# A state-space and mLSTM decoder block on one core: one rotation table for four batches, an earlier weight ring, and weight sums laid out by rows

## The chip, the core and the metric

The kernel runs on one core of a Trainium2 chip. The core has a matrix engine (TensorE, PE in the profile, with PEld for the loading of its weights), VectorE (DVE), ScalarE (ACT), GpSimd (POOL) and SyncE (SP), and 16 DMA engines that move data between the chip's main memory and on-chip memory. Each engine works its instructions in program order and waits on semaphores for the others. The metric is the device time of one execution, in microseconds (us).

## What is computed

One decoder block on 1024 positions of width 1024, with 16 learned positions in front, all in float32. Cut to what matters:

```python
h = layer_norm(concat([meta, x]), ln0_g, ln0_b)
p = h @ w_in + b_in
u_s5, q, k, v, o_pre, i_pre, f_pre, g_s5, g_m = split(p)
y_s5 = s5(u_s5, ...)                      # 32 groups x 64 complex states: x_t = A x_{t-1} + B u_t, y_t = Re(C x_t) + D u_t
z = gelu(y_s5) @ s5_w_glu
y_s5 = z[:, :1024] * sigmoid(z[:, 1024:])
...
y_m = (sigmoid(o_pre) * head_norm(mlstm(conv_silu(q, k), v, i_pre, f_pre))) @ m_w_out
mix = sigmoid(g_s5) * y_s5 + sigmoid(g_m) * y_m
h = layer_norm(alpha * h + mix @ w_o)
h = layer_norm(alpha * h + relu(h @ w_up + b_up) ** 2 @ w_down)
```

## The kernel before

**Matrix products.** Every float32 product is made of three passes (mm3, L226 to L228): both operands are split into a high part, rounded to the PE's fast format, and a low part, the remainder. For a weight tile of 128 x 1024 the load is L198 (wraw, from SP), the high part whi is a copy by ACT (L212) and the low part wlo a subtraction by DVE (L213). The first pass uses whi (L226), the second whi with the low part of the input (L227), the third wlo (L228).

**Jobs.** The first half of the block is a list of jobs, ORDER: q and k, v, o (output gates of the mLSTM), u (input of the state-space layer S5, four jobs u0 to u3), g (gates of S5), m (two of the mLSTM's gate tiles), and then z0 to z7 (the GLU product on gelu(y_s5)). A job is one or two weight tiles and some 48 matmuls; weights are loaded two jobs ahead and split one job ahead, with high priority. The rest of the gates (three pairs of tiles) and the mLSTM's output product come after z7 as stages of seven products in place of eight (class Seven), then the output projection, a layer norm and the feed-forward part.

**Side work.** S5, mLSTM, convolution and the residual scaling are generators in lanes ("s5c", "s5", "s5g", "ml", "cv", "ah"); mm3 pumps them between matmuls by a running estimate of PE time, and a yield states what a step is thought to cost. A scheduler then sets the order of the instructions on each engine, by priorities; from there each engine goes through its own queue in order, so an instruction that stands late in DVE's queue waits for all ahead of it.

**S5.** The 32 groups run as four batches b of four group pairs (q runs over 16 pairs). When the job of S5_START begins, s5_pre computes powers of the transition. When job u_b is done, s5_consts(b) and s5_batch(b) are queued. s5_consts builds the input and output matrices (L699 to L741) and a table T of 130 rotations for each of its four pairs, by doubling: seven complex products of 4, 8, 16, 32, 64, 128 and 256 columns and one more of 4, each of six DVE operations (cmul, L572 to L577, through the tile s5tt). s5_batch multiplies the input by a matrix (L802, PE), copies the result out (L810), rotates it by T (L817 to L823), runs the recurrence as a scan (L828), rotates back (L838 to L841), puts the halves together (L846) and multiplies by the output matrix (L857, L858, PE). The result goes through main memory (ys_dr, L863; s5yc, L871), and s5_gelu applies gelu and splits it into gelh and gell (L877, L878), which z0 to z7 multiply.

**Residual scaling and early up-projection.** At job g4 ah_scale is queued (ahr in by L1377, two DVE products L1386, out by L1388), and behind it up_early, which computes a part of the feed-forward weights' combinations (L1412, L1413) and stores them (wu_dr, L1414).

**The seam after z7.** When z7 begins, the pool mid is closed and a pool ring is opened in its place, with three buffers of two weight tiles for the stages of seven products. begin() issues eight loads of the normalised input (rawb, L991). After z7, first() loads three ring buffers (Seven.load, L1024), splits the first (Seven.split: whi L1042, wlo L1043) and forms the sums and differences of input blocks (sub, L1002; to_home, L997 and L998). Four of the seven products need sums of weight blocks; w_sums has POOL's DMAs compute them in main memory (ws_dr, L974), one DMA in every second job, some adding into the destination.

Of the kernel before, what the change touches and what calls it, by code (L numbers as in the profile page):

```python
# [38 lines left out]
LN2_2 = math.log(2.0) - LN2_1  # L39
MAGIC = 1.5 * 2 ** 23  # L40
ORDER = "q0 q1 v0 q2 v1 q3 o1 o0 v2 o2 o3 u0 u1 v3 u2 g0 u3 g1 o4 o5 o7 o6 g2 g3 g5 g6 g4 g7 m0 m1"
S5_START = "u0"
NM = 2
SPLIT_UP = 200
PRE = 3
# [67 lines left out]
def decoder_block(  # L113
# [80 lines left out]
    def load_w(job):  # L194
        job.raw = []
        for src, n in job.loads:
            r = slot("wraw") if ring[0] is None else ring[0].tile([P, 1024], F32, tag="wr", bufs=3, name="wraw")
            nc.sync.dma_start(r[:, :n], src)  # L198
            job.raw.append(r)

# [378 lines left out]
    def s5_pre():  # L579
# [89 lines left out]
             v3(tm[:, 0:256]), v3(tm[:, 256:512]))  # L669
        yield 1.3  # L670

    GEL = {}

    def s5_consts(b):
# [83 lines left out]
                g_.dma_start(mx[16 * j:16 * j + 16, :, g2, 16 * j:P],  # L758
                              kt[16 * g2:16 * g2 + 16, :, 0:P - 16 * j])
        yield K5[b]  # L760
        T = slot("s5T")
        tc_, ts_ = (T[:, i * 520:(i + 1) * 520].rearrange("p (q c) -> p q c", q=4) for i in range(2))
        tmp = slot("s5tt")
        g_.memset(tc_[:, :, 0], 1.0)
        g_.memset(ts_[:, :, 0], 0.0)
        g_.tensor_copy(tc_[:, :, 1], S5["p8"][:, 0, q0:q0 + 4])
        g_.tensor_copy(ts_[:, :, 1], S5["p8"][:, 1, q0:q0 + 4])
        yield C5[b]
        n = 1
        while n < 129:  # L770
            m = min(n, 129 - n)
            sh = [P, 4, m]
            w1 = tmp[:, 0:4 * m].rearrange("p (q c) -> p q c", q=4)
            w2 = tmp[:, 512:512 + 4 * m].rearrange("p (q c) -> p q c", q=4)
            cmul(v_, tc_[:, :, n + 1:n + 1 + m], ts_[:, :, n + 1:n + 1 + m], tc_[:, :, 1:m + 1], ts_[:, :, 1:m + 1],
                 tc_[:, :, n:n + 1].to_broadcast(sh), ts_[:, :, n:n + 1].to_broadcast(sh), w1, w2)
# [181 lines left out]
    def w_sums():  # L958
        todo = {}
        for s, (n0, p0, w, i0) in enumerate(((3, 0, wf, JGM + NM), (4, 3, wmo, 0))):  # L960
            def src(r, kh):
                return bass.AP(tensor=w.tensor, offset=w.offset + (i0 + r) * KT * P * P + 512 * kh,
                               ap=[[2 * KT * P * P, n0], [KT * P, P], [1, 512]])
            a11, a12, a21, a22 = src(0, 0), src(0, 1), src(1, 0), src(1, 1)
            d = [ws_dr[p0:p0 + n0, i] for i in range(4)]
            todo[s] = [(d[0], a21, 0), (d[2], a11, 0), (d[0], a22, 1), (d[2], a21, 1), (d[1], d[0], 0), (d[1], a11, 1),
                       (d[3], d[1], 0), (d[3], a12, 1)]
        mark = const.tile([1, 1], F32, name="mark")
        for s, i in ((0, 0), (0, 1), (0, 2), (0, 3), (0, 4), (1, 0), (0, 5), (1, 1), (0, 6), (1, 2), (0, 7), (1, 3),
                     (1, 4), (1, 5), (1, 6), (1, 7)):  # L970
# [33 lines left out]
    class Seven:  # L1004
# [8 lines left out]
        def load(self, i):  # L1013
            if i >= self.ntile():
                return
            r = ring[0].tile([P, 1024], F32, tag="wr", bufs=3, name="wraw")
            for j, (n, p) in enumerate(self.units[2 * i:2 * i + 2]):
                s = {5: 0, 6: 1, 7: 2, 3: 3}.get(n)
                if s is None:
                    t = self.w[self.i0 + 2 * p + (n == 4)].rearrange("p k f -> p (k f)")  # L1020
                    a = t[:, 0:512] if n == 1 else t[:, 512:1024]
                else:
                    a = ws_dr[self.p0 + p, s]
                tc.keep_in_program_order(nc.sync.dma_start(r[:, j * 512:j * 512 + 512], a))  # L1024
            self.raw[i] = r
# [117 lines left out]
    def gates_and_output():  # L1143
# [6 lines left out]
            for nm, kh, ch in (("12", 0, 1), ("22", 1, 1), ("11", 0, 0), ("21", 1, 0)):  # L1150
                R[nm] = raw_block(h_dr, kh, ch, META)

        def first():
            for i in range(3):
                g.load(i)
            g.split(0)
            sub(R["22"], R["12"], R["22"])
            sub(R["12"], R["12"], R["11"])
# [919 lines left out]
```

## Time and profile before

| | before |
|---|---|
| median of 3 runs | 1566.78 us (1564.85 to 1566.83) |
| profiled execution | 1566.04 us, span 1564.2 us |
| mean granted clock of TensorE | 0.984 |
| matmuls | 7593 |
| DVE instructions | 2083 |

The span is what the profiler recorded between the first and the last instruction; 1.84 us of that execution lie around it. A row of the page by slices cuts the span in 40 equal parts of 39.1 us and gives busy tenths of each engine:

```profile
PE   8999999998999998989999999999999999999997
DVE  7667555659867845677789675666666679766786
PEclk9999999998999999989999999999999999999999
DMA  8412324414354556775353328644443798667642
```

The granted clock falls to 0.8 in the tenth slice (352 to 391 us) and in the eighteenth (665 to 704 us), and PE's busy share is lowest there and in the sixteenth (587 to 626 us). The windows further on look into these three places.

### The profile page before, as it was taken

What the parts mean: (1) busy time and instruction counts of PE and PEld (TensorE: products, weight loads), DVE (VectorE), ACT (ScalarE), POOL (GpSimd) and SP (SyncE); (2) the same over time, 40 slices, a digit from 0 to 9 for tenths busy, and PEclk for the clock granted to TensorE, in tenths of its full rate; (3) what the DMA queues carried; (4) which work ended last, traced back from release to release, by engine and by line L of the source; (5) the groups of instructions that cost most, each with busy time, mean ns of one, the idle gap of its engine ahead of it and who ended that gap; (6) DMA issues with size and microseconds to landing.
All of it is one profiled execution on the core that took longest, in us unless ns stands there. A gap on an engine that the chain in (4) does not pass through costs nothing.

```text
span 1564.2 us, 20543 instructions
## 1 busy us (share of the span) xinstructions
PE 1515.8 (97%) x7593; PEld 1278.7 (82%) x7593; DVE 1079.9 (69%) x2083; ACT 642.7 (41%) x982; POOL 102.2 (7%) x195
## 2 busy tenths in 40 slices
PE   8999999998999998989999999999999999999997
PEld 8998988996878886768788887888888888888886
DVE  7667555659867845677789675666666679766786
ACT  6523353333355433325534324444444534433340
POOL 0000001124031200000000001000000000000000
PEclk9999999998999999989999999999999999999999
DMA  8412324414354556775353328644443798667642
GB/s 311 159 57 61 100 62 129 122 37 112 104 129 103 164 182 218 279 269 195 108 170 114 108 76 247 225 158 149 147 149 123 248 363 322 230 229 236 216 166 108
DMA packets 137509, 261.32 MB, mean 167 GB/s; under 512 B 30768, under 2 KB 52984, under 8 KB 137352
## 3 DMA queue, kind: packets, MB, share of 16 engines
q1 hardware_dynamic: 111344, 233.00, 43.7%
q0 software_dynamic: 26064, 27.01, 7.1%
q8 instruction: 60, 0.98, 0.3%
q14 instruction: 41, 0.34, 0.1%
HBM read 188.78 MB, written 84.55 MB: 175 GB/s over the span
## 4 chain that ended last, share of the span: by engine, by line
PE 31%; issue 23%; DMA 3%; DVE 2%; ACT 0%; SPq 0%; POOL 0%; POOLq 0%; DVEq 0%
PE mm L228 7%; PE mm L227 7%; PE mm L226 7%; PE sd L227 3%; PE sd L226 3%; PE sd L228 3%; DMA wpre<-wu_dr 1%; DMA rawb<-h_dr 1%; DMA wu_dr<-wpre 1%; DMA wur<-in_wup_dram 0%; DVE wlo L1043 0%; DVE wlo L213 0%; DMA woraw<-in_wo_dram 0%; POOL wpre L1621 0%; SPq L991 0%
## 5 line engine op out<-in xcount | busy, mean ns | idle before, releaser
L226 PE MATMUL mm<-hT_hi,whi 128*128 128x512 f32 (+3 forms) x604 | 231.0, 382 | 8.0 <-ACT whi L1042 5.4
L228 PE MATMUL mm<-hT_hi,wlo 128*128 128x512 f32 (+3 forms) x604 | 226.7, 380 | 5.7 <-DVE wlo L213 3.7
L227 PE MATMUL mm<-hT_lo,whi 128*128 128x512 f32 (+3 forms) x604 | 229.1, 379 | 0.0
L226 PEld LDWEIGHTS mm<-hT_hi,whi 128*128 128x128 f32 x604 | 115.7, 192 | 26.6 <-ACT whi L1042 6.2
L228 PEld LDWEIGHTS mm<-hT_hi,wlo 128*128 128x128 f32 x604 | 115.0, 191 | 25.5 <-DVE wlo L213 4.3
L227 PEld LDWEIGHTS mm<-hT_lo,whi 128*128 128x128 f32 x604 | 115.6, 191 | 17.6 <-issue 0.4
L227 PE MATMUL sd<-dwl,dah 128*128 128x512 f32 x240 | 94.5, 394 | 0.0
L228 PE MATMUL sd<-dwh,dal 128*128 128x512 f32 x240 | 94.4, 394 | 0.0
L226 PE MATMUL sd<-dwh,dah 128*128 128x512 f32 x240 | 94.2, 393 | 0.0
L1773 ACT ACTIVATE dah<-da 128x1024 fp32r<-128x1024 f32 x56 | 58.7, 1052 | 86.2 <-PE sd L227 38.9
L1777 ACT ACTIVATE dwh<-wdr 128x1024 fp32r<-128x1024 f32 x56 | 58.9, 1053 | 84.0 <-DMA wdr<-in_wdn_dram 27.5
L1774 DVE TENSOR_TENSOR dal<-da,dah 128x1024 fp32r<-128x1024 f32 x56 | 68.2, 1219 | 23.8 <-ACT dah L1773 23.3
L228 PE MATMUL mm<-dwh,dal 128*128 128x512 f32 (+1 forms) x224 | 84.5, 378 | 0.0
L226 PE MATMUL mm<-dwh,dah 128*128 128x512 f32 (+1 forms) x224 | 84.4, 377 | 0.0
L227 PE MATMUL mm<-dwl,dah 128*128 128x512 f32 (+1 forms) x224 | 84.3, 377 | 0.0
L1778 DVE TENSOR_TENSOR dwl<-wdr,dwh 128x1024 fp32r<-128x1024 f32 x56 | 68.2, 1219 | 13.1 <-ACT dwh L1777 12.4
L226 PE MATMUL mm<-whi,hT_hi 128*128 128x256 f32 (+1 forms) x256 | 75.2, 294 | 0.0
L228 PE MATMUL mm<-whi,hT_lo 128*128 128x256 f32 (+1 forms) x256 | 74.7, 292 | 0.0
L227 PE MATMUL mm<-wlo,hT_hi 128*128 128x256 f32 (+1 forms) x256 | 73.8, 288 | 0.0
L213 DVE TENSOR_TENSOR wlo<-wraw,whi 128x1024 fp32r<-128x1024 f32 (+1 forms) x46 | 56.1, 1222 | 19.1 <-ACT whi L212 18.6
L228 PE MATMUL mm<-th,wul 128*128 128x512 f32 x156 | 61.6, 395 | 0.0
L227 PE MATMUL mm<-tl,wuh 128*128 128x512 f32 x156 | 61.5, 394 | 0.0
(474 smaller groups left out, 3703.1 us busy)
## 6 DMA issues: line engine op xcount, KB each, us to landing
da<-act_dr SPq DMA_DIRECT2D x56, 512.0 KB, 5.4
wdr<-in_wdn_dram SPq DMA_DIRECT2D x56, 512.0 KB, 6.3
wur<-in_wup_dram SPq DMA_DIRECT2D x32, 512.0 KB, 4.3
act_dr<-upy SPq DMA_DIRECT2D x64, 256.0 KB, 2.5
wraw<-in_wf_dram SPq DMA_DIRECT2D x30, 512.0 KB, 6.9
wu_dr<-wpre SPq DMA_DIRECT2D x21, 512.0 KB, 4.7
wpre<-wu_dr POOLq DMA_DIRECT2D x21, 512.0 KB, 5.0
act_dr<-upx SPq DMA_DIRECT2D x32, 256.0 KB, 2.8
```

What stands on the lines that cost most here:

```text
L213: todo.append(lambda e=v_, r=r, hi=hi, lo=lo, n=n: e.tensor_tensor(lo[:, :n], r[:, :n], f32(hi[:, :n]), op=OP.subtract))
L226: t_.matmul(ps, ah, bh, start=(i == 0 and part[0]), stop=False, skip_group_check=skip)
L227: t_.matmul(ps, ah, bl, start=False, stop=False, skip_group_check=skip)
L228: t_.matmul(ps, al, bh, start=False, stop=(i == n - 1 and part[1]), skip_group_check=skip)
L1773: a_.activation(ah[:, :D], a[:, :D], AF.Copy)
L1774: v_.tensor_tensor(alo[:, :D], a[:, :D], f32(ah[:, :D]), op=OP.subtract)
L1777: a_.activation(wh, raw[i], AF.Copy)
L1778: v_.tensor_tensor(wl, raw[i], f32(wh), op=OP.subtract)
```

## The change

It has four parts.

1. The job that starts s5_pre is o2 in place of u0, three jobs earlier. Behind s5_pre stands a new generator s5_table, which builds one table of 66 rotations for all 16 pairs, by products of 16, 32, 64, 128, 256, 512 and 16 columns, once. Each batch copies its 66 columns with two ACT copies and makes the other 64 with one product of 256 columns.
2. The pool ring is opened at z4, four jobs earlier, and has four buffers. GLU weights no longer use it. The first three ring loads (early()) are issued at z6; begin() stays at z7, and first() stays after z7 without its loads.
3. The access patterns of the weight sums have the 128 rows as the outermost dimension, in place of the 3 or 4 pairs.
4. The program is built with a descriptor memory of 4096 bytes for GpSimd's DMAs (dynamic_dma_scratch_size).

```diff
-S5_START = "u0"
+S5_START = "o2"
...
     def load_w(job):
...
-            r = slot("wraw") if ring[0] is None else ring[0].tile([P, 1024], F32, tag="wr", bufs=3, name="wraw")
+            r = slot("wraw")
...
+    def s5_table():
+        S5["T"] = T = mid.tile([P, 2, 16, 66], F32, name="s5_T")
+        tm, (c, s) = slot("s5tt"), (T[:, 0], T[:, 1])
+        g_.memset(c[:, :, 0], 1.0)
+        g_.memset(s[:, :, 0], 0.0)
+        g_.tensor_copy(c[:, :, 1], S5["p8"][:, 0])
+        g_.tensor_copy(s[:, :, 1], S5["p8"][:, 1])
+        yield 1.3
+        n = 1
+        while n < 65:
+            m = min(n, 65 - n)
+            sh = [P, 16, m]
+            cmul(v_, c[:, :, n + 1:n + 1 + m], s[:, :, n + 1:n + 1 + m], c[:, :, 1:m + 1], s[:, :, 1:m + 1],
+                 c[:, :, n:n + 1].to_broadcast(sh), s[:, :, n:n + 1].to_broadcast(sh),
+                 *(tm[:, i * 512:i * 512 + 16 * m].rearrange("p (q c) -> p q c", q=16) for i in range(2)))
+            n *= 2
+            yield 1.3
...
         yield K5[b]
-        T = slot("s5T")
+        T, tmp = slot("s5T"), slot("s5tt")
+        t1, s1 = S5["T"][:, 0, q0:q0 + 4], S5["T"][:, 1, q0:q0 + 4]
...
-        g_.memset(tc_[:, :, 0], 1.0)
-        g_.memset(ts_[:, :, 0], 0.0)
-        g_.tensor_copy(tc_[:, :, 1], S5["p8"][:, 0, q0:q0 + 4])
-        g_.tensor_copy(ts_[:, :, 1], S5["p8"][:, 1, q0:q0 + 4])
+        a_.activation(tc_[:, :, 0:66], t1, AF.Copy)
+        a_.activation(ts_[:, :, 0:66], s1, AF.Copy)
+        sh = [P, 4, 64]
+        cmul(v_, tc_[:, :, 66:130], ts_[:, :, 66:130], t1[:, :, 2:66], s1[:, :, 2:66],
+             t1[:, :, 64:65].to_broadcast(sh), s1[:, :, 64:65].to_broadcast(sh),
+             *(tmp[:, i * 512:i * 512 + 256].rearrange("p (q c) -> p q c", q=4) for i in range(2)))
         yield C5[b]
-        n = 1
-        while n < 129:
...
-            n *= 2
-            yield C5[b]
...
-                               ap=[[2 * KT * P * P, n0], [KT * P, P], [1, 512]])
+                               ap=[[KT * P, P], [2 * KT * P * P, n0], [1, 512]])
...
-            d = [ws_dr[p0:p0 + n0, i] for i in range(4)]
+            d = [ws_dr[p0:p0 + n0, i].rearrange("n p c -> p n c") for i in range(4)]
...
-            r = ring[0].tile([P, 1024], F32, tag="wr", bufs=3, name="wraw")
+            r = ring[0].tile([P, 1024], F32, tag="wr", bufs=4, name="wraw")
...
-        def first():
+        def early():
             for i in range(3):
                 g.load(i)
+
+        def first():
             g.split(0)
...
         if j.tag == S5_START:
             lanes["s5c"].add(s5_pre())
+            lanes["s5c"].add(s5_table())
...
-        if j.tag == "z7":
+        if j.tag == "z4":
             mid_ctx.close()
             ring_ctx = ExitStack()
             ring[0] = ring_ctx.enter_context(tc.tile_pool(name="ring", bufs=1, side="left"))
+        if j.tag == "z6":
+            early()
+        if j.tag == "z7":
             begin()
...
-    nc = _bacc.Bacc("TRN2", target_bir_lowering=False, num_devices=1)
+    nc = _bacc.Bacc("TRN2", target_bir_lowering=False, num_devices=1, dynamic_dma_scratch_size=4096)
```

Three places show what this does to the engines' queues. The lines of the changed kernel are 10 to 12 higher than those of the kernel before for the same statement (L820 for L810, L763 for L745).

**DVE, around the first S5 batch.** Before, these rows end with u3's wlo; ahead of them stand the last table step, L817 to L820 and L719. The s5w and s5Z rows are batch 0, gB and dec belong to the mLSTM.

```order
L828 SCALAR_TENSOR_TENSOR s5w<-s_r_3019,s5Z 128x130 x4
L444 SCALAR_TENSOR_TENSOR gB<-gB,acol,mask 128x128 x3
L828 SCALAR_TENSOR_TENSOR s5w<-s_r_3019,s5Z 128x130 x4
L444 SCALAR_TENSOR_TENSOR gB<-gB,acol,mask 128x128 x5
L838 TENSOR_TENSOR s5Z<-s5w,s5T 128x512
L841 TENSOR_TENSOR s5w<-s5w,s5T 128x512
L450 COPY dec<-wiB 128x9
L745 SCALAR_TENSOR_TENSOR s5Kt<-s_eye,s_d,s5Kt 32x16 x2
L839 TENSOR_TENSOR s5w<-s5w,s5T 128x512
L840 TENSOR_TENSOR s5Z<-s5w,s5T 128x512
L745 SCALAR_TENSOR_TENSOR s5Kt<-s_eye,s_d,s5Kt 32x16 x2
L213 TENSOR_TENSOR wlo<-wraw,whi 128x1024
```

In the changed kernel the same work of batch 0 (L827 to L830, L737, L832, L833 and the eight scans L838 are just ahead of these rows) ends with the wlo of g0, one job ahead of u3:

```order
L848 TENSOR_TENSOR s5Z<-s5w,s5T 128x512
L851 TENSOR_TENSOR s5w<-s5w,s5T 128x512
L492 TENSOR_SCALAR dd<-pn 128x1
L849 TENSOR_TENSOR s5w<-s5w,s5T 128x512
L850 TENSOR_TENSOR s5Z<-s5w,s5T 128x512
L497 BN_STATS hst<-hraw 128x6
L493 SCALAR_TENSOR_TENSOR dd<-pn,ecol,dd 128x1
L763 SCALAR_TENSOR_TENSOR s5Kt<-s_eye,s_d,s5Kt 32x16 x4
L856 TENSOR_TENSOR s5w<-s5Z,s5w 64x512 x4
L498 BN_AGGR hmv<-hst 128x2
L495 RECIPROCAL dd<-dd 128x1
L213 TENSOR_TENSOR wlo<-wraw,whi 128x1024
```

The table step is gone from the queue, the mLSTM's L444 has moved behind, and L856, which stood behind the wlo at L846, now stands ahead of a wlo, that of the job before. On PE 16 matmuls of u2 (128x400), six of the mLSTM, eight transposes s5p and eight products s5k stand between the last s5z of batch 0 and g0's first matmul, and four matmuls between that and g0's first use of wlo.

**SP, from the last S5 batch to the GLU jobs.** Before, the batch's output is stored (ys_dr) and read back (s5yc) inside the chain of the residual scaling (ahr and ah_dr):

```order
L1377 DMA ahr<-ah_dr 128x1024
L1388 DMA ah_dr<-ahr 128x1024
L1377 DMA ahr<-ah_dr 128x1024
L198 DMA wraw<-in_wf_dram 128x1024
L1377 DMA ahr<-ah_dr 128x1024 x2
L198 DMA wraw<-in_wglu_dram 128x1024
L1388 DMA ah_dr<-ahr 128x1024
L863 DMA ys_dr<-s5Y 128x1024
L1388 DMA ah_dr<-ahr 128x1024
L871 DMA s5yc<-ys_dr 16x8x128 x8
L1377 DMA ahr<-ah_dr 128x1024
L1388 DMA ah_dr<-ahr 128x1024
```

In the changed kernel both stand ahead of that chain:

```order
L873 DMA ys_dr<-s5Y 128x1024
L881 DMA s5yc<-ys_dr 16x8x128 x8
L198 DMA wraw<-in_wf_dram 128x1024 x2
L1384 DMA gB_5536<-in_ln0r_dram 128x1024
L1384 DMA bB_5537<-in_ln0r_dram 128x1024
L1389 DMA ahr<-ah_dr 128x1024 x2
L198 DMA wraw<-in_wf_dram 128x1024
L1389 DMA ahr<-ah_dr 128x1024
L1400 DMA ah_dr<-ahr 128x1024 x3
L1389 DMA ahr<-ah_dr 128x1024
L198 DMA wraw<-in_wglu_dram 128x1024
```

On PE the last batch's final s5y pair stands at the end of job g3 now and stood at the end of g4 before: three jobs, or 39 us of PE work when the matmuls between are counted at their durations in the trace.

**SP and DVE at the seam.** Before, on SP (in_wf weights for the first three ring buffers, ws_dr sums for the next three):

```order
L198 DMA wraw<-in_wglu_dram 128x1024
L1414 DMA wu_dr<-wpre 128x1024 x7
L991 DMA rawb<-h_dr 128x2x512 x8
L1024 DMA wraw<-in_wf_dram 128x512 x6
L1024 DMA wraw<-ws_dr 128x512 x6
```

After:

```order
L1426 DMA wu_dr<-wpre 128x1024 x6
L1034 DMA wraw<-in_wf_dram 128x512 x6
L1426 DMA wu_dr<-wpre 128x1024
L1001 DMA rawb<-h_dr 128x2x512 x8
L1034 DMA wraw<-ws_dr 128x512 x6
```

The weights have moved ahead of the rawb loads and of the last wu_dr store. On DVE before, where L944 and L945 drain the last GLU jobs:

```order
L1002 TENSOR_TENSOR rawb<-rawb 128x1024 x3
L944 TENSOR_TENSOR z2s<-mm,z2s 128x512
L1002 TENSOR_TENSOR rawb<-rawb 128x1024 x2
L945 TENSOR_TENSOR sgs<-z2s,sgs 128x512
L944 TENSOR_TENSOR z2s<-mm,z2s 128x512
L1002 TENSOR_TENSOR rawb<-rawb 128x1024
L998 TENSOR_TENSOR hT_lo<-rawb,hT_hi 128x2x512
L1002 TENSOR_TENSOR rawb<-rawb 128x1024
L945 TENSOR_TENSOR sgs<-z2s,sgs 128x512
L1043 TENSOR_TENSOR wlo<-wraw,whi 128x1024
```

After, with L954 and L955 for these:

```order
L1053 TENSOR_TENSOR wlo<-wraw,whi 128x1024
L955 TENSOR_TENSOR sgs<-z2s,sgs 128x512
L1012 TENSOR_TENSOR rawb<-rawb 128x1024 x2
L954 TENSOR_TENSOR z2s<-mm,z2s 128x512
L1012 TENSOR_TENSOR rawb<-rawb 128x1024
L955 TENSOR_TENSOR sgs<-z2s,sgs 128x512
L1012 TENSOR_TENSOR rawb<-rawb 128x1024 x2
L1053 TENSOR_TENSOR wlo<-wraw,whi 128x1024
L1012 TENSOR_TENSOR rawb<-rawb 128x1024 x2
L1008 TENSOR_TENSOR hT_lo<-rawb,hT_hi 128x2x512
```

The first wlo now stands ahead of all L1012 (which was L1002), the second behind five of them, where before the first stood behind seven.

More of the change, by code (lines that the diff above doesn't have):

```diff
@@ L760, in s5_consts @@
         yield K5[b]
-        T = slot("s5T")
+        T, tmp = slot("s5T"), slot("s5tt")
+        t1, s1 = S5["T"][:, 0, q0:q0 + 4], S5["T"][:, 1, q0:q0 + 4]
         tc_, ts_ = (T[:, i * 520:(i + 1) * 520].rearrange("p (q c) -> p q c", q=4) for i in range(2))
-        tmp = slot("s5tt")
-        g_.memset(tc_[:, :, 0], 1.0)
-        g_.memset(ts_[:, :, 0], 0.0)
-        g_.tensor_copy(tc_[:, :, 1], S5["p8"][:, 0, q0:q0 + 4])
-        g_.tensor_copy(ts_[:, :, 1], S5["p8"][:, 1, q0:q0 + 4])
-        yield C5[b]
-        n = 1
-        while n < 129:
[L771 to L776, printed above, removed]
-            n *= 2
-            yield C5[b]
+        a_.activation(tc_[:, :, 0:66], t1, AF.Copy)
[4 more added lines that the diff above has]
+             *(tmp[:, i * 512:i * 512 + 256].rearrange("p (q c) -> p q c", q=4) for i in range(2)))
+        yield C5[b]
         S5["m", b] = (RS, Mi, Mx, T)
@@ L1189, in run @@
             y.run(lambda c, p: sdps() if c == "b" and p else mmps(), ym_evac, yhooks)
-        return begin, first, run
+        return early, begin, first, run
     def ln0_load(t):
@@ L1467, in decoder_block @@
     next(ws)
-    begin, first, run7 = gates_and_output()
+    early, begin, first, run7 = gates_and_output()
     for i, j in enumerate(jobs):
```

## The prediction

> **What bounds the kernel now.** The first page shows the engine that sets the pace:
>
> ```profile
> PE 1515.8 (97%) x7593; PEld 1278.7 (82%) x7593; DVE 1079.9 (69%) x2083; ACT 642.7 (41%) x982; POOL 102.2 (7%) x195
> ```
>
> PE (TensorE) is busy in 97% of the span, so a change that takes no matmul away can win only where PE waits or runs at a lowered clock. The next view is therefore PE's waits between 340 and 720 us, the part of the span that the change touches (columns: total wait, times, longest):
>
> ```profile
> PE mm L226 <- ACT whi L1042: 5.4, 1, 5.4
> PE mm L228 <- DVE wlo L213: 4.9, 4, 3.7
> PE mm L227 <- DVE gell L878: 3.1, 1, 3.1
> ...
> PE s5k L741 <- DVE s5Ri L719: 2.9, 1, 2.9
> PE mm L226 <- DVE z2s L944: 2.1, 1, 2.1
> PE mm L228 <- DVE wlo L1043: 1.9, 1, 1.9
> ```
>
> They fall into three places. A wait costs more than its length, since the granted clock drops; the windows view shows both (columns: window, length, busy us of PE, PEld, DVE, ACT, POOL, granted clock, DMA share, GB/s):
>
> ```profile
> 360.00:400.00 40.00, 32.31 (x179) 28.61 (x178) 37.92 (x129) 18.74 (x30) 19.07 (x23) 0.83 0.40 109
> 370.00:375.00 5.00, 2.13 (x15) 1.67 (x14) 4.96 (x12) 0.21 (x1) 2.02 (x4) 0.90 0.52 140
> 375.00:380.00 5.00, 3.37 (x10) 2.16 (x9) 5.00 (x16) 4.67 (x8) 5.00 (x1) 0.50 0.35 78
> 380.00:385.00 5.00, 1.81 (x8) 1.81 (x9) 4.95 (x14) 3.12 (x4) 5.00 (x6) 0.50 0.16 30
> 385.00:390.00 5.00, 5.00 (x33) 5.00 (x32) 4.42 (x25) 0.00 (x0) 4.18 (x9) 0.73 0.48 124
> 595.00:600.00 5.00, 1.85 (x7) 1.21 (x6) 3.60 (x4) 0.50 (x2) 0.00 (x0) 0.93 0.62 227
> 600.00:605.00 5.00, 3.99 (x12) 2.77 (x10) 2.11 (x2) 1.53 (x3) 2.08 (x2) 0.73 0.65 204
> 605.00:610.00 5.00, 3.88 (x10) 3.12 (x11) 4.06 (x6) 0.00 (x0) 0.00 (x0) 0.66 0.80 172
> 685.00:690.00 5.00, 4.26 (x19) 3.13 (x17) 4.31 (x5) 0.00 (x0) 0.00 (x0) 1.00 1.05 388
> 690.00:695.00 5.00, 0.35 (x1) 0.35 (x2) 5.00 (x6) 2.11 (x2) 0.00 (x0) 0.65 1.05 385
> 695.00:700.00 5.00, 3.09 (x7) 1.97 (x7) 5.00 (x6) 1.06 (x1) 0.00 (x0) 0.50 0.12 18
> 700.00:705.00 5.00, 5.00 (x19) 3.96 (x18) 1.62 (x2) 1.57 (x3) 0.00 (x0) 0.83 0.25 96
> ```
>
> PE's busy time times its clock is the work done at full speed; the rest of each window is lost. **Place 1**, job u3 (370 to 390): 1.92 + 1.69 + 0.91 + 3.65 = 8.2 of 20, lost 11.8 us; VectorE (DVE) is the cause, busy 37.92 of 40 us there. **Place 2**, the first GLU job z0 (595 to 610): 1.72 + 2.91 + 2.56 = 7.2 of 15, lost 7.8. **Place 3**, the seam from the last GLU job to the seven-product gates (685 to 705): 4.26 + 0.23 + 1.55 + 4.15 = 10.2 of 20, lost 9.8. Together 29.4 us are at stake.
>
> **Place 1: one table, begun earlier.** The tile of the rotation products shows what the tables cost now, all four batches together, and the DVE timeline what a step costs:
>
> ```profile
> 340.00:620.00 280.00, 37.86 (x192) 0.96 0.50 142
> ...
> 366.39 0.42 DVE L572 TENSOR_TENSOR s5tt<-s5T 128x256 f32<-128x256 f32 x1
> ...
> 368.89 0.17 DVE L572 TENSOR_TENSOR s5tt<-s5T 128x4 f32<-128x4 f32 x1
> ```
>
> A batch has 48 products in 37.86 / 4 = 9.5 us; its 256-column step takes 368.89 - 366.39 = 2.5. The new table drops the steps of 4, 8 and 4 columns (18 x 0.17 = 3.1) and gains a second one of 16 (6 x 0.17 = 1.0, the price of 4 columns) and one of 512 (6 x 0.67 = 4.0, by L838's row below): 11.4 us, once. Each batch keeps one step like the 256-column one. After: 11.4 + 4 x 2.5 = 21.4, so DVE does 16.4 us less. ScalarE (ACT) gets eight copies of 264 columns, GpSimd (POOL) loses 12 small operations; both have room (18.74 and 19.07 of 40 us in the first window).
>
> But PE waits for no table; it waits for wlo, the low part of a weight tile, and DVE works its queue in order. What stood ahead of u3's wlo:
>
> ```profile
> 359.93 0.29 DVE L810 COPY s5Z<-s5z 64x130 f32<-64x130 f32 x1
> ...
> 369.53 0.69 DVE L817 TENSOR_TENSOR s5w<-s5Z,s5T 128x520 f32<-128x520 f32 x1
> ...
> 372.17 0.75 DVE L719 SCALAR_TENSOR_TENSOR s5Ri<-s5tm 128x576 f32<-128x576 f32 x1
> ...
> 374.20 1.37 DVE L828 TENSOR_TENSOR_SCAN s5w<-s_r,s5Z 128x130 f32<-128x130 f32 x4
> ...
> 378.86 0.67 DVE L838 TENSOR_TENSOR s5Z<-s5w,s5T 128x512 f32<-128x512 f32 x1
> ...
> 381.93 1.21 DVE L213 TENSOR_TENSOR wlo<-wraw,whi 128x1024 fp32r<-128x1024 f32 x1
> ...
> 383.32 2.79 DVE L846 TENSOR_TENSOR s5w<-s5Z,s5w 64x512 f32<-64x512 f32 x4
> ```
>
> From the last s5Z copy to u3's wlo went 22 us, table included. In the changed order batch 0 ends one job earlier and g0's wlo stands behind all of it, L846's four too: 4 of L817's kind (2.5), L719 (0.7), 2 sums (1.2), 8 scans (2.7), 4 of L838's kind (2.5), 4 small L745 (0.6), L846 (2.8), mLSTM scraps (1.3), wlo itself (1.2): 15.5 us, and the two copies ahead of it 0.6. PE meanwhile has, by its order, 16 matmuls of 400 columns, 16 small S5 ones, a few of the mLSTM and g0's first four. Its spacing:
>
> ```profile
> 364.14 0.40 PE L226 MATMUL mm<-hT_hi,whi 128*128 128x512 f32 x1
> 364.38 0.39 PE L227 MATMUL mm<-hT_lo,whi 128*128 128x512 f32 x1
> ```
>
> At 0.23 us per 512 columns that is 2.9 + 2.0 + 0.6 + 0.9 = 6.4 us. So PE stalls about 9 us at g0. The clock adds what it added elsewhere: at place 3 waits of 7.3 cost 9.8, at place 1 waits of 7.7 cost 11.8; I add 2.5. **The stall moves from u3 to g0 and keeps its size, 11.5 for 11.8.** The DVE time saved lies off PE's path, and the table itself fits between o2 and v3, where PE's waits were short. Small waits at g1 and o4, behind batches 1 and 2, are as likely as the disappearance of small ones of before: net gain 0.5 us. Bounds: -6 (two more waits of 3) to +9 (g0's stall covered by PE work that overtakes).
>
> **Place 2.** z0 waited for gell, the low part of the last S5 batch, and this is why it was late:
>
> ```profile
> 573.88 10.98 SPq L871 DMA_DIRECT2D s5yc<-ys_dr  x8
> ...
> 597.42 1.22 DVE L878 TENSOR_TENSOR gell<-gelf,gelh 128x1024 fp32r<-128x1024 f32 x1
> ```
>
> Between them stood loads and stores of the residual scaling (ah) on SyncE (SP) and their products on DVE. In the changed order the last batch's y stands 39 us of PE work earlier, and on SP its loads are issued ahead of the whole ah chain. Even if the ah products run late, gell is done by then; z2s, the second wait, stands behind them no more. **Gain 7.8**; bounds 5 (the 2.1 and its share of clock stay) to 8.
>
> **Place 3.** The seam is a DMA queue:
>
> ```profile
> 676.63 6.08 SPq L991 DMA_DIRECT2D rawb<-h_dr  x8
> 682.75 6.99 SPq L1024 DMA_DIRECT2D wraw<-in_wf_dram  x6
> ...
> 685.41 3.96 DVE L1002 TENSOR_TENSOR rawb<-rawb 128x1024 f32<-128x1024 f32 x3 [5.75 <-DMA rawb<-h_dr]
> ...
> 693.54 1.06 ACT L1042 ACTIVATE whi<-wraw 128x1024 fp32r<-128x1024 f32 x1 [1.35 <-DMA wraw<-in_wf_dram]
> 697.36 1.22 DVE L1043 TENSOR_TENSOR wlo<-wraw,whi 128x1024 fp32r<-128x1024 f32 x1
> ```
>
> The first gate weights were asked for behind 4 MB of rawb at 385 GB/s. Now they go ahead of all of it and of one wu_dr store. Their split is then done before z7 ends (PE fell idle at 694.65 - 5.39 = 689.3), and the 24 matmuls of tile 0 run at once (5.5 us). But 1.5 MB ahead at 385 GB/s put the last rawb, and L1002's first subtraction, 4 us later, at 689.4; and in DVE's changed order five L1002 (5.7) and two drains of z7 (1.2) stand between it and wlo of tile 1, which ends at 697.5 where PE wants it at 695.8; wlo of tile 2 comes 8 us later behind six more large operations, at 705.5, wanted at 703.1. Loss 1.7 + 2.4 = 4.1 in place of 9.8: **gain 5.6.** I charge no clock, since neither wait is as long as the 3.1 us after which 0.73 was granted at z0; with the 2.5 us that place 3 pays now the gain is 3. Bounds 2 to 10. By the Trainium skill (TensorE: Matmul & The Clock Gate, Part 1) it takes an idle window of about 3.4 us to halve the clock; the 5.39 us wait, with 0.65 and 0.50 granted behind it, agrees, and by that rule too the seam pays no clock.
>
> **Weight sums.** Nothing on PE waits for them now:
>
> ```profile
> wraw<-in_wf_dram SPq DMA_DIRECT2D x30, 512.0 KB, 6.9
> ...
> ws_dr<-in_wmo_dram POOLq DMA_DIRECT2D x6, 1024.0 KB, 29.1
> ```
>
> 1024 KB in 29.1 us against 512 KB in 6.9 say that a sum uses few engines. Rows outermost, it may spread over all: finished sooner, but in the way of a weight load for some us; loads are asked for two jobs (over 20 us) ahead, so I cost it at nothing, bounds -3 to 0. The smaller descriptor memory gets nothing either: no row of before shows a wait for it.
>
> **Rivals.**
> - **A, g0's stall stays away** because u2 runs later than the order suggests and DVE catches up: 1552.1 - 11 = 1541. Against it: the same queue gave u3 its stall. 0.15.
> - **B, the seam gives it all back**: clock and later rawb cost 9.8 again: 1552.1 + 5.6 = 1558. For it: 385 GB/s is all that queue gets. 0.13.
> - **C, slower**: g0's mechanism repeats at g1 and o4, where batches 1 and 2 now stand ahead of wlo (19 us of DVE for some 13 of PE at each, by the prices above). Two stalls of 11 give 1552.1 + 22 = 1574; from 14 us on, all is lost. Against it: a tile split ahead leaves some 8 us of slack before them. 0.09.
> - **D, the change does not bring S5 forward in time**, g0's stall passing on to each batch, and z0 waits as before: 1552.1 + 7.8 = 1560. 0.08.
> - **E, sums in the way**: twelve transfers, 6 of 1 MB and 6 of 0.75 MB, now take the whole 385 GB/s for 2 to 2.7 us each; where half of them delay a late load, and POOL's own late loads pay too, 12 to 14 us go: 1565. 0.05. By the Trainium skill (DMA: Bandwidth & Descriptors, why a semaphore rises by 16, and issuing engines) a pattern led by 3 or 4 rows uses 3 or 4 of the 16 engines, one led by 128 all 16, and queues of all issuers share them; the 29.1 us agree with the first, and no run yet shows the second.
>
> **How the numbers follow.** The profiled execution took 1566.04 us (span 1564.2 and 1.84 around it), 0.74 under the median of 1566.78, so I sum against it: 1566.04 - 0.5 - 7.8 - 5.6 = 1552.1. Chance 0.50, with its own bounds about 1546 to 1557. The range 1540 to 1561 takes in A, B and D and leaves out C and E. What a measurement can tell from no change is about 0.2%, 3.1 us: faster 0.50 + 0.15 + 0.13 + 0.08 = 0.86, same 0.05 (E), slower 0.09 (C).
>
> **What would show it.** Place 1: a wait of 8 to 10 us of PE for wlo L213 some 12 us of PE work ahead of where u3's was, with the clock at 0.50, and 21 us in the products' tile for 37.86. Place 2: no PE wait on gell or z2s, clock 1.00 through z0. Place 3: PE waits of about 2 us on the seam's second and third wlo, the first L1002 about when z7 ends. A PE wait on whi L212 or wraw in 200 to 480 us would speak for E. The forecast is wrong if g0's wait is under 4 us or comes three times.

## The result and the profile after

The changed kernel took 1554.27 us (median of 4, 1553.72 to 1555.77) against 1566.22 (median of 4, 1564.85 to 1566.83): a ratio of 0.9926, 95% interval 0.9912 to 0.9939. 1552.1 had been forecast, so the total was hit within 2.2 us. The steps were not: the runs below show a gain of about 16 us where nothing was put down, and a loss of about 10 where half a microsecond of gain was.

The first page of the changed kernel has the matmuls unchanged and 126 DVE instructions fewer (1957 for 2083). POOL has 12 fewer and ACT 9 more:

```profile
PE 1512.1 (97%) x7593; PEld 1276.9 (82%) x7593; DVE 1063.6 (68%) x1957; ACT 646.8 (42%) x991; POOL 88.2 (6%) x183
```

PE's waits of the changed kernel between 340 and 720 us (total, times, longest) show which waits have gone and which are new. The 5.4 us on the seam's whi and the waits on gell and z2s are gone. The waits on whi L212 and wlo L213 now lie at g0 and at two later jobs, one on s5Z and three on kw of the mLSTM have come, and the one on hraw (1.7 before) has stayed:

```profile
PE mm L226 <- ACT whi L212: 5.2, 3, 2.2
PE mm L228 <- DVE wlo L213: 5.2, 2, 3.1
PE mm L228 <- DVE wlo L1053: 3.4, 2, 2.0
PE pS L463 <- ACT kw L460: 2.6, 3, 1.9
PE s5z L812 <- DVE s5Z L820: 2.5, 1, 2.5
PE pt L513 <- DVE hraw L506: 1.6, 1, 1.6
```

The windows of the changed kernel (columns as in the prediction) show place 1, the new losing stretches behind it, z0's and the seam's:

```profile
345.00:350.00 5.00, 4.31 (x25) 3.87 (x25) 4.60 (x10) 0.87 (x2) 0.00 (x0) 1.00 0.31 99
350.00:355.00 5.00, 3.44 (x24) 2.55 (x22) 5.00 (x16) 2.01 (x5) 0.00 (x0) 1.00 0.01 6
355.00:360.00 5.00, 2.08 (x4) 1.17 (x4) 4.93 (x15) 4.91 (x10) 3.94 (x8) 0.59 0.48 92
360.00:365.00 5.00, 3.82 (x9) 3.05 (x10) 4.89 (x17) 1.31 (x4) 1.94 (x4) 0.50 1.05 331
365.00:370.00 5.00, 5.00 (x20) 3.95 (x20) 0.82 (x3) 0.00 (x0) 3.72 (x8) 0.89 0.65 183
...
440.00:450.00 10.00, 7.89 (x37) 5.93 (x36) 9.97 (x22) 4.95 (x11) 0.00 (x0) 0.83 0.00 0
...
510.00:515.00 5.00, 2.83 (x8) 1.62 (x7) 4.63 (x9) 2.48 (x4) 1.79 (x2) 0.50 0.88 262
...
560.00:600.00 40.00, 40.00 (x174) 32.47 (x173) 21.78 (x18) 7.34 (x10) 1.88 (x2) 1.00 0.68 237
600.00:640.00 40.00, 40.00 (x175) 32.50 (x175) 20.84 (x30) 13.12 (x20) 1.43 (x2) 1.00 0.68 212
...
680.00:720.00 40.00, 36.60 (x157) 28.87 (x156) 30.95 (x31) 19.84 (x23) 0.00 (x0) 1.00 0.73 258
```

Read as before, length less busy time times clock, place 1 (345 to 370) lost 9.7 us of 25: done were 4.31 + 3.44 + 1.23 + 1.91 + 4.45 = 15.3. The GLU jobs lost nothing, and the seam 3.4.

The same sum over windows of 5 us, for the kernels that matter most, is the map for all that follows (us lost by PE; the experiments are explained below):

| stretch | before | after | sums only (e1) | early start only (e4) | change, late start (e6) | change without table (e5) |
|---|---|---|---|---|---|---|
| 120 to 160 | 6.7 | 2.9 | 2.9 | 4.3 | 1.0 | 0.8 |
| 320 to 400 (place 1) | 13.5 | 11.5 | 14.1 | 5.7 | 4.5 | 12.3 |
| 400 to 520 | 4.1 | 20.2 | 4.1 | 16.9 | 16.1 | 5.2 |
| 560 to 640 (place 2) | 7.9 | 0.0 | 0.0 | 7.2 | 0.0 | 0.0 |
| 640 to 720 (place 3, GLU) | 12.6 | 3.4 | 8.7 | 17.5 | 3.4 | 3.3 |
| 0 to 1520, all | 55.1 | 47.9 | 40.3 | 60.3 | 36.2 | 32.0 |

The map finds 7.2 us (55.1 less 47.9) of the 10.4 by which the span fell from 1564.2 to 1553.8; some 3 us of that are not located. Two rows lie outside the sum of the forecast: 120 to 160 us, and the 16.1 us of new losses between 400 and 520, which only rival C had in view.

### The profile page after: what moved, and what is told of

The parts are those of the page before. It is cut to its first block, busy times and chain, and to the rows that moved or that the text cites. A ratio compares the mean times of both kernels' runs of the same rounds, so it can differ in the third digit from the quotient of the medians.

```text
span 1553.8 us, 20411 instructions
## 1 busy us (share of the span) xinstructions
PE 1512.1 (97%) x7593; PEld 1276.9 (82%) x7593; DVE 1063.6 (68%) x1957; ACT 646.8 (42%) x991; POOL 88.2 (6%) x183
## 4 chain that ended last, share of the span: by engine, by line
PE 73%; issue 16%; DVE 6%; ACT 3%; DMA 1%; SPq 0%; POOLq 0%; DVEq 0%; ACTq 0%
PE mm L228 18%; PE mm L226 18%; PE mm L227 18%; PE sd L227 4%; PE sd L226 4%; PE sd L228 4%; PE mm L1317 2%; PE mm L1325 1%; PE pu L477 1%; PE pn L473 1%; PE pn L474 1%; DMA wiB<-wrow_dr 1%; DVE s5w L838 1%; PE pt L513 0%; PE ln L1581 0%
## 5 line engine op out<-in xcount | busy, mean ns | idle before, releaser
L213 DVE TENSOR_TENSOR wlo<-wraw,whi 128x1024 fp32r<-128x1024 f32 (+1 forms) x46 | 56.0, 1221 | 56.2 <-ACT whi L212 47.4
```

The source lines that it names most:

```text
L213: todo.append(lambda e=v_, r=r, hi=hi, lo=lo, n=n: e.tensor_tensor(lo[:, :n], r[:, :n], f32(hi[:, :n]), op=OP.subtract))
```

## The experiments

Each is compared with the kernel before in runs on the same chip; its four medians there were 1566.09 (e1 to e4), 1565.94 (e5 to e8), 1565.88 (e9 to e11) and 1564.97 (e12).

### The parts one by one

**e1: only the weight sums with rows outermost.**

```diff
-                               ap=[[2 * KT * P * P, n0], [KT * P, P], [1, 512]])
+                               ap=[[KT * P, P], [2 * KT * P * P, n0], [1, 512]])
-            d = [ws_dr[p0:p0 + n0, i] for i in range(4)]
+            d = [ws_dr[p0:p0 + n0, i].rearrange("n p c -> p n c") for i in range(4)]
```

> The kernel before with the weight sums' rows outermost and nothing else. Theory (the sums, on few DMA engines, hold back a 24 KB load that VectorE waits for at 117 us): about 3.8 us less than before, 1562.4; VectorE's wait for s_lam (3.6 us before) and PE's wait on gps at 124 us (2.0) gone, a sum of 1024 KB in 10 us instead of 29, the waits at u3, z0 and the seam as before. Rival (the early gain comes from the smaller descriptor memory, or from chance): 1566.2, s_lam waited for as before.

Measured: 1550.51 us (1548.37 to 1551.11), ratio 0.9898 [0.9883, 0.9913], 15.6 us less. Its own expectation, 1562.4 with z0 and the seam as before, was far off. This part alone brings more than the whole change does. The transfers between 520 and 640 us show why (queue, count, KB each, median us from issue to landing). Kernel before:

```profile
ah_dr<-ahr SPq DMA_DIRECT2D x8, 512.0 KB, 6.6
...
wraw<-in_wf_dram SPq DMA_DIRECT2D x2, 512.0 KB, 12.2
...
ws_dr<-in_wmo_dram POOLq DMA_DIRECT2D x2, 1024.0 KB, 33.6
```

With the sums alone:

```profile
ah_dr<-ahr SPq DMA_DIRECT2D x8, 512.0 KB, 3.0
...
wraw<-in_wf_dram SPq DMA_DIRECT2D x2, 512.0 KB, 5.9
...
ws_dr<-in_wmo_dram POOLq DMA_DIRECT2D x2, 1024.0 KB, 10.2
```

A sum fell from 33.6 us to 10.2, and other transfers, which nothing in the edit touches, landed in half their time: the stores ah_dr and the weight loads of in_wf. Not all gained as much in that stretch: ahr took 6.0 us for 6.9 and wu_dr 4.5 for 4.7. That the layout of the sums alone changed the landing times is measured. Why is argued: if a sum keeps a few DMA engines busy, a transfer that is spread over all of them is as late as its share on those few. The traces do not tell the single engines apart. The last S5 batch shows it on the path. The queue of SP, and the tile of gell (instruction numbers, first and last start), with the sums alone:

```profile
562.91 5.45 SPq L871 DMA_DIRECT2D s5yc<-ys_dr  x8
```

```profile
L878 DVE TENSOR_TENSOR gell<-gelf,gelh x4: 1218/1224/1225, 431.5 to 584.0; 128x1024 fp32r<-128x1024 f32 x4
```

s5yc is issued at 562.91 for 573.88, takes 5.45 us to issue for 10.98, and gell starts at 584.0 for 597.42, although PE has the last batch's products at the same place of its order as before. z0 waits no more, and place 2's 7.9 us are gone. One more wait goes that the prediction had not looked at. DVE before, between 95 and 126 us, waited for 24 KB of S5 constants:

```profile
DVE s_t L557 <- DMA s_lam<-in_s5l_dram: 3.6, 1, 3.6
```

PE stood behind it at 120 to 130 us; with the sums alone that load lands in time (3.8 us less lost in the map's first row). And POOL before waited at two of its s5Mx transfers for a sum to land:

```profile
POOL s5Mx L758 <- DMA ws_dr<-in_wmo_dram: 16.9, 2, 13.9
```

That row is gone too. The seam and the GLU jobs together lost 8.7 for 12.6. The three gains of the map, 3.8 + 7.9 + 3.9, add up to the 15.6 measured, but the map is a coarse gauge. PE's last matmul starts 18.4 us sooner than before (1536.97 for 1555.34 us), and the end behind it is 3.3 us longer, since the span (1549.1 us for 1564.2) falls by 15.1 only. e2 shows more of that.

**e2: the sums and the descriptor memory of 4096 bytes.** The order of the instructions is that of e1 on every engine.

```diff
+    nc = _bacc.Bacc("TRN2", target_bir_lowering=False, num_devices=1, dynamic_dma_scratch_size=4096)
```

> The same with the descriptor memory of 4096 bytes. Theory: the memory costs and gains nothing, so the time of the run with the sums alone, within 1 us. Rival (smaller memory holds POOL's transfers back): slower than that by 1 to 4 us, with PE waiting on wpre loads near 940 us. Rival (the memory brings the early gain): 3.8 us faster than that.

Measured: 1545.43 us (1544.21 to 1546.89), ratio 0.9868 [0.9853, 0.9883]: 5.1 us less than e1, with ranges apart, where no difference over 1 us had been expected. In the two profiled executions most of it lies behind PE's work. PE's last matmul starts at 1536.97 us in e1 and at 1535.11 in e2, 1.9 us sooner, and from there to the end of the span it is 12.1 us in e1 and 8.8 in e2. What takes longer is GpSimd's DRAIN at the end of the program (count, then the shortest, median and longest in ns, then first and last start). First e1, then e2:

```profile
L2074 POOLq DRAIN  x3: 46/98/6500, 1541.8 to 1548.8; - x3
```

```profile
L2074 POOLq DRAIN  x3: 46/98/2908, 1540.0 to 1543.7; - x3
```

The kernel before, with the same memory as e1 and the old sums, has the short end too, and no other kernel here is over 9.1 us. Why is open, and whether every execution of e1 had it, since one was profiled. No row puts the other 1.9 us down to the memory. At 145 to 150 us the clock was 0.66 in e1, behind a wait of 1.24 us on kw, and 1.00 in e2, behind one of 0.99. But e10 below, with the memory of 4096 bytes, has 0.66 there as well, behind 1.20. In the first 40 us e2 lost 8.3 us for e1's 10.3, but e5, with that memory, lost 10.1, and e4, without it, 8.3.

**e3: only the ring, opened at z4 with four buffers and loaded at z6** (the lines of part 2 of the change).

> The kernel before with the ring opened at z4, four buffers and the early weight loads, and nothing else. Theory (the seam is a term of its own): about 6 us less than before, 1560; PE's wait on whi of 5.4 us at the seam gone, two waits on wlo of 1.3 to 2.0 there; gell (3.1) and z2s (2.1) at z0 as before. Rival (the ring also makes the GLU jobs' waits of 2.8 us between 640 and 680 go): 1557.

Measured: 1559.83 us (1558.32 to 1562.53), ratio 0.9965 [0.9949, 0.9981], 6.3 us less. The wait of 5.4 on the seam's whi is gone, the two on its wlo make 3.3, and PE waits for gell (2.4 us for 3.1) and z2s (2.1) much as before. From 680 to 720 us the kernel lost 4.4 for 9.8, a gain of 5.4 where 5.6 was forecast.

**e4: only the early start, with the old tables.**

```diff
-S5_START = "u0"
+S5_START = "o2"
```

> The kernel before with S5_START at o2 and nothing else, so the old tables are built per batch. Theory (not the earlier start but the shorter tables bring the last batch forward; by the order its last product moves by 2 us of PE work only): 1564 to 1569, gell waited for at z0 as before. Rival (the earlier start alone brings S5 forward): 1556 to 1559, no wait on gell.

Measured: 1574.26 us (1572.73 to 1575.48), ratio 1.0051 [1.0036, 1.0066], 8.2 us more and outside both expectations. Place 1 shrinks from 13.5 to 5.7 us, but 12.8 come up between 400 and 520, and 4.9 between 640 and 720. From 340 to 720 us PE waits 8.9 us in six pieces on whi L212, where the kernel before had 3.0 in four.

### The change less one part

**e5: the change without its first part**, old tables and old start (u0).

```diff
-S5_START = "o2"
+S5_START = "u0"
...
-    def s5_table():
...
-            lanes["s5c"].add(s5_table())
```

> Sums, memory and ring of the change; table and start as before. Theory (from the runs of the parts: the table begun at o2 costs what the sums win, and the ring's 6.3 us add up): 1545.4 - 5 to 6 = 1540, and the wait of u3 as before, no wait on gell, seam waits of 2 us. Rival (the sums and the ring win the same us at the seam, so they don't add): 1544 to 1546. Rival (the table is worth its DVE time and the change's parts merely overlap): not under 1552.

Measured: **1542.39 us** (1541.44 to 1544.0), ratio 0.9853 [0.9839, 0.9868]. It beats both kernels, by 23.6 us and by about 12, lies between its two expectations, and is the fastest here together with e10, whose median lies inside its range.

**e6: the whole change, but started at u0 as before.**

```diff
-S5_START = "o2"
+S5_START = "u0"
```

> The whole change with S5_START back at u0 (table kept). Theory (the table itself is no harm, the early start is: it packs batch 0 ahead of g0's wlo and leaves the last batches and the mLSTM bunched at o6 and g2): 1540 to 1545, PE's waits at g0 (5.2), at 443 (2.1) and at 505 to 516 us (5.4) at most half as long. Rival (the table, which takes a buffer's room and DVE time before the first batch, is the cost): 1552 to 1556.

Measured: 1544.25 us (1542.91 to 1545.06), ratio 0.9863 [0.9849, 0.9878]. The table itself does no harm that can be told from noise: the intervals of e5 and e6 overlap. The early start costs the other 10 us (1554.27 against 1544.25). PE's waits of e6, 340 to 720 us, show that the stall at the first gate job is gone, and what came in its place:

```profile
PE pt L513 <- DVE hraw L506: 6.7, 2, 4.4
PE mm L228 <- DVE wlo L1053: 3.4, 2, 2.0
PE s5p L751 <- DVE s5Z L820: 2.8, 1, 2.8
PE mm L226 <- ACT whi L212: 2.8, 1, 2.8
```

Place 1 lost 4.5 us for 13.5, and 400 to 520 lost 16.1 for 4.1. So what PE gains at the first batch is lost again 100 us later, most of it at the mLSTM's head normalisation. The longer of the two waits on hraw (4.4 us, ending at 474.91) has an S5 batch ahead of it in DVE's queue, from 457.21 us to these rows:

```profile
469.15 1.39 DVE L856 TENSOR_TENSOR s5w<-s5Z,s5w 64x512 f32<-64x512 f32 x2
...
474.44 1.38 DVE L506 TENSOR_SCALAR hraw<-hraw,hmv,hny 128x256 f32<-128x256 f32 x4 [0.24 <-DVE hny L176]
```

**e7: the whole change without the ring.**

> The change without its ring part: table, start at o2, sums and memory. Theory (ring worth 6.3 us by itself): 1554.3 + 6.3 = 1560.6; place 1 with its stall at g0 as in the changed kernel, no wait on gell. Rival (ring opened at z4 forces the mid pool closed early and hurts or helps the GLU jobs): more than 2 us off that.

Measured: 1558.37 us (1557.26 to 1559.25), ratio 0.9954 [0.9938, 0.9971]; the ring is worth 4.1 us inside the change (1558.37 less 1554.27), with whi L1052 waiting 3.3 at the seam again. Beside e2 and e5, without the early start, it is worth 3.0 (1545.43 less 1542.39), alone 6.3: the sums take away a part of the same wait (5.4 before, 3.0 in e1).

**e8: the kernel before with a descriptor memory of 8192 bytes**, same order on every engine.

```diff
+    nc = _bacc.Bacc("TRN2", target_bir_lowering=False, num_devices=1, dynamic_dma_scratch_size=8192)
```

> The kernel before with a descriptor memory of 8192 bytes and nothing else; the instructions stand in the same order. Theory (size alone does nothing, the 5 us between the first two runs are a matter of when small waits meet the clock): 1563 to 1569. Rival (a smaller memory makes POOL's transfers or all others cheaper): 1561.

Measured: 1571.65 us (1568.94 to 1572.88), ratio 1.0036 [1.0023, 1.0049], 5.7 us more, against both expectations. POOL's waits, 60 to 620 us, have a row that showed 0.7 us before:

```profile
POOL ws_dr L974 <- issue: 8.8, 3, 7.4
```

POOL stood 7.4 us, up to 497.71 us, at a sum that it could not issue. PE lost 8.4 us between 400 and 520 us, where the kernel before lost 4.1; that the one caused the other is not shown. With the sums on few engines the smaller memory costs; with rows outermost (e2) an even smaller one did not. 4096 bytes with the old sums was not tried.

### The loss at the gate jobs

**e9: the change, with the first batch's halves (L856) put together on GpSimd.** Three microseconds of DVE ahead of g0's wlo go away.

```diff
-                v_.tensor_tensor(w1[64 * i:64 * i + 64, 512 * g2:512 * g2 + 512], Z[r, c], w2[r, c], op=op)
+                (g_ if b == 0 else v_).tensor_tensor(w1[64 * i:64 * i + 64, 512 * g2:512 * g2 + 512], Z[r, c], w2[r, c], op=op)
```

> The changed kernel with the four L856 of batch 0 (2.8 us of DVE) on GpSimd, so that they no longer stand ahead of g0's wlo in VectorE's queue. Theory (g0's wlo is late by what stands ahead of it in that queue): PE's wait for it falls from 3.1 us to about 0.3, with less of the low clock behind it; 2.5 to 5 us off 1554.3: 1549 to 1552. Rival (the wlo is late because its weight tile, whose load was issued at 347 us only, lands late): the wait stays at 3 us, time 1553 to 1556. Whi's wait of 2.2 us stays in both.

Measured: 1557.99 us (1557.16 to 1558.61), ratio 0.9946 [0.9932, 0.9961], 3.7 us more than the change and above both expectations (the ranges of the times are apart, the intervals of the two ratios just touch). DVE's timeline around g0's wlo, first in the changed kernel:

```profile
345.48 0.30 DVE L820 COPY s5Z<-s5z 64x130 f32<-64x130 f32 x1 [0.34 <-ACT s5Z L822]
...
356.39 0.65 DVE L763 SCALAR_TENSOR_TENSOR s5Kt<-s_eye,s_d,s5Kt 32x16 f32<-32x16 f32 x4
356.97 2.78 DVE L856 TENSOR_TENSOR s5w<-s5Z,s5w 64x512 f32<-64x512 f32 x4
359.92 1.20 DVE L213 TENSOR_TENSOR wlo<-wraw,whi 128x1024 fp32r<-128x1024 f32 x1
```

then in e9, with GpSimd's row behind it:

```profile
356.16 2.28 DVE L763 SCALAR_TENSOR_TENSOR s5Kt<-s_eye,s_d,s5Kt 32x16 f32<-32x16 f32 x4
358.51 1.19 DVE L213 TENSOR_TENSOR wlo<-wraw,whi 128x1024 fp32r<-128x1024 f32 x1
361.83 1.39 DVE L575 TENSOR_TENSOR s5tt<-s_T 128x256 f32<-128x256 f32 x1
```

```profile
355.32 7.61 POOL L856 TENSOR_TENSOR s5w<-s5Z,s5w 64x512 f32<-64x512 f32 x4 [21.01 <-ACT s5RS L767]
```

The wlo came 1.4 us sooner, not 3: while GpSimd worked, DVE's four L763 took 2.28 us for 0.65. The four halves took 7.61 us for 2.78, and POOL's s5Mx transfers stood behind them. Even so place 1 lost 10.6 us for the change's 11.5, so the 3.7 us are not lost there. The seam lost 4.7 for 3.4: it has the same waits on wlo, but the clock was 0.76 from 700 to 705 us. The rest is not located.

**e10 and e11: the change with start u0 and gate jobs moved ahead of o6**, to give PE work while the mLSTM waits.

```diff
-ORDER = "... o4 o5 o7 o6 g2 g3 g5 g6 g4 g7 m0 m1"
+ORDER = "... o4 o5 o7 g2 o6 g3 g5 g6 g4 g7 m0 m1"
```

(e11 has "o7 g2 g3 o6 g5".)

> The change with S5_START at u0 and ORDER with g2 between o7 and o6. Theory (the loss of 11 us near 475 us in the run with the late start is the last mLSTM head run out by itself ahead of o6, and work of another job covers it): PE's wait of 4.4 us on hraw L506 gone or under 1.5, 4 to 8 us off 1544.3: 1536 to 1540. Rival (the hold-up only moves with o6, VectorE being the bound): 1543 to 1546.

> The same with g2 and g3 between o7 and o6. Theory: as with g2 alone or 1 to 2 us better, 1534 to 1540. Rival (VectorE the bound): 1543 to 1546.

Measured: 1543.11 us (1541.17 to 1545.01), ratio 0.9852 [0.9837, 0.9866], and 1544.18 (1540.79 to 1544.52), 0.9853 [0.9836, 0.9869]. Neither can be told from e6, as the rivals expected, and e10's wait on hraw is still there (7.2 us in two pieces, 6.7 in e6).

**e12: start u0, with the mLSTM's steps told as cheaper**, so that they are pumped more closely.

```diff
-ML = [2.4, 1.2, 1.68, 4.8]
+ML = [2.4, 1.2, 1.2, 2.4]
```

> The change with S5_START at u0 and the planner's steps of the last two mLSTM heads shortened, ML [2.4, 1.2, 1.68, 4.8] to [2.4, 1.2, 1.2, 2.4], so that on PE 7 and 10 us of other matmuls stand between a head's last pn and its transposes pt, where the runs with the late start have next to nothing there. Theory (a chain of small steps through ScalarE and VectorE, some 5 us long, lies bare): PE's waits on hraw of 6.7 us fall under 1.5, 6 to 10 us off 1544.3: 1534 to 1538, faster than the changed kernel by about 18 and than the run without the table by 5. Rival (VectorE's total work between u3 and g2 is the bound, and a wait on wlo or whi takes their place): 1542 to 1547.

Measured: 1550.55 us (1550.02 to 1551.52), ratio 0.9911 [0.9895, 0.9928], 6.3 us more than e6 and above both expectations. The wait on hraw halves, and others take its place:

```profile
PE mm L226 <- ACT whi L212: 4.5, 3, 2.8
PE pt L513 <- DVE s5Z L820: 3.9, 1, 3.9
PE pt L513 <- DVE hraw L506: 3.4, 1, 3.4
```

Moving work between PE and its partners in this stretch moves the wait. That is what a stretch bound by the chain through DVE would do; it was not shown by taking DVE work away there.

## Why the prediction was right in its number and wrong in its steps

Added up by the runs: sums 15.6 less, memory beside them 5.1 less, ring beside both 3.0 less, table 1.9 more (inside the intervals), early start 10.0 more. That makes 11.8 less, and 12.0 was measured (1566.22 less 1554.27). The forecast was 13.9. Two of its own terms come out a little larger than it wrote them: 15.5 + 0.6 less 6.4 is 9.7 at g0, not about 9, and 9.8 less 4.1 is 5.7 at the seam, not 5.6.

- **Weight sums: costed at nothing, worth 15.6 us.** This is the step that failed most. "Nothing on PE waits for them" was true and the wrong question: PE waited for transfers that the sums held up. The row that was quoted, 29.1 us for 1024 KB, held the hint. The bounds ran from -3 to 0 and left out any gain, for which no reason was given.
- **Place 2: the gain of 7.8 was right, but S5's lead was not needed for it.** e1 takes the whole of it with S5 where it was. The forecast read the order on SP rightly and missed that the transfers in it were slow. Whether the lead alone would have been enough is not shown: the changed kernel has both, and its last gell starts at 554.2 us for 597.42, as early as forecast. e4 starts S5 early without the sums, but there the last gell still starts at 598.5 us (as late as before), and place 2 lost 7.2 us, with PE waiting 4.3 for a sigmoid (sgm L952) that stands behind the gelu in ACT's queue.
- **Place 1: the loss at the first stall came near its forecast, but as two waits; its successors were left out.** DVE needed 15.6 us from the last s5Z copy (345.48) to the end of g0's wlo (361.12), where 15.5 + 0.6 had been added up. The stall cost 9.7 for a forecast 11.5. One wait of 8 to 10 us on wlo had been forecast, and under 4 us was to speak against it; PE waited for whi first and then 3.06 us for wlo:

```profile
356.05 0.80 PE L226 MATMUL mm<-hT_hi,whi 128*128 128x512 f32 x1 [2.19 <-ACT whi L212]
...
361.18 0.79 PE L228 MATMUL mm<-hT_hi,wlo 128*128 128x512 f32 x1 [3.06 <-DVE wlo L213]
```

  The whi goes back to DVE as well: in ACT's queue it stood behind hraw L496, which waited 2.51 us for DVE's L495, an instruction behind the scans. So the queue was the right cause, and the way through ACT was missed. The products' tile between 270 and 620 us came out as worked out, 21.28 us for 21.4:

```profile
270.00:620.00 350.00, 21.28 (x66) 0.96 0.46 130
```

- **The early start: put at +0.5 with a bound of -6, cost 10.** e6 against the changed kernel shows the cost. Rival C, given 0.09, named the mechanism, though at 22 us it was too large: batches 1 and 2 hold up later weights too. The forecast's own test, a wait that "comes three times", came true: whi and wlo at 356 to 361, whi at 443, whi and wlo at 511 to 516. The second of them was not quite the queue that C had in mind. PE wanted whi, and ACT's row in its own waits, 340 to 520 us, names what whi stood for:

```profile
ACT whi L212 <- DVE s5Ri L737: 4.2, 1, 4.2
```

L737 is the last reader of a scratch tile of the S5 batch that comes from the same set of 30 buffers as whi, so the trace points to a buffer that DVE gave back late; no run tested that. Of the third, ACT's timeline shows a part: between the copies of batch 2's s5Z stood a change of function table (1.28 us, from 504.85) and two output gates (1.26 us, L898).

- **Place 3: right in mechanism and size.** In the changed kernel's DVE and PE timelines the first subtraction starts at 686.18, and the second and third wlo are waited for 1.35 and 2.04 us, forecast 1.7 and 2.4:

```profile
694.33 0.50 PE L228 MATMUL mm<-hT_hi,wlo 128*128 128x512 f32 x1 [1.35 <-DVE wlo L1053]
...
702.28 0.50 PE L228 MATMUL mm<-hT_hi,wlo 128*128 128x512 f32 x1 [2.04 <-DVE wlo L1053]
```

  The stretch from 680 lost 3.4 us, 4.1 being forecast, and the clock stayed at 1.00, as charged. The clock was luck in part: e9 has the same 2.03 us on the third wlo, and behind it the clock was 0.76. Of the gain of 6.4 the sums alone would have brought a part (e1 lost 8.7 for 12.6 from 640 to 720 us).
- **Descriptor memory: nothing put down, 5.1 us measured beside the sums.** In the profiled executions 3.3 of it lie at the end, behind PE's last matmul, which is longer in e1 than in every other kernel here. The cause is open.
- **Rival E** (sums in the way, 0.05) had the sign wrong: with rows outermost the sums cost the others less, not more. It counted twelve of them; the page of the changed kernel has sixteen. Its sign, a wait on whi between 200 and 480 us, did appear (4.3 us for 1.3 before), but with the early start and not with the sums: e4, with the old sums, has 2.7, and e1 and e2 have 1.3.

So the total agreed by luck: a gain of about 16 us that was half put down to another cause and half missed, with the 5 us that came with the memory on top, met a loss of 10 that was missed as well.

## What to carry to other kernels

A transfer that nothing waits for can still set the pace: if its row shows several times the landing time of others of its size, suspect that it keeps a few DMA engines busy and look at the landing times of everything else beside it. When work is moved earlier, follow the whole of it, to the last batch: here the first stall shrank a little and later ones grew behind the next batches. And take a change of several parts apart even when the total comes out as forecast: three of the four parts give 1542 us where all four give 1554.

## What the runs showed of the hardware that was not expected

- **Transfers that nothing waits for can make others late.** Beside sums led by 3 or 4 pairs some 512 KB transfers took twice as long to land between 520 and 640 us (12.2 us for 5.9, 6.6 for 3.0), others hardly longer (6.9 for 6.0, 4.7 for 4.5). By the Trainium skill (DMA: Bandwidth & Descriptors, why a semaphore rises by 16) a pattern led by 128 rows takes all 16 engines; the other half of the rule that rival E quoted now agrees as well, as far as the landing time tells. Over a whole run the six 1024 KB sums of the changed kernel land in 9.8 us, 29.1 before.

- **The descriptor memory can change the time with an unchanged order of instructions.** With 8192 bytes and the old sums POOL stood 7.4 us at one issue; with 4096 beside the new sums the kernel took 5.1 us less, and GpSimd's last DRAIN 2.91 us for 6.50.
- **GpSimd's elementwise work and DVE's held each other up in turn (e9):** DVE's L763 took 2.28 us for 0.65, and L575, whose like takes 0.41 when undisturbed in the same timeline, 1.39. The wlo between them, also of two inputs, kept its 1.19, and it was GpSimd's third half, beside it, that took 3.17 us, where the other three took 1.26 to 1.61.
- **One wait well under 3 us can halve the clock, and an equal one need not.** In the changed kernel the four matmuls behind the wait of 2.49 us on s5Z take 1.20 us, where four of the same shape (L513, at 499.84 us) took 0.60, and the clock from 510 to 515 us was 0.50:

```profile
508.84 0.69 PE L812 MATMUL s5z<-s5U,s5Mi 128*128 128x130 f32 x4 [2.49 <-DVE s5Z L820]
509.56 1.20 PE L867 MATMUL s5y<-s5U,s5Mx 128*128 128x128 f32 x4
```

  Behind a wait on kw of 1.20 us in e10 the clock from 145 to 150 us was 0.66, behind one of 1.16 in e11 it was 1.00. The Trainium skill (TensorE: Matmul & The Clock Gate, Part 1) gives an idle window of about 3.4 us; here no single wait was that long, so single waits are no safe measure.
